# A two-layer block on one Trainium2 core: ranking in the routing stage, weight slabs by number, the last LN's rows spread by PE, the last halves one by one

## The chip, the cores and the metric

The kernel runs on one core of one Trainium2 chip. The metric is the device time of one execution in microseconds (us); lower is better. The engines are called as in the profile: PE (TensorE's matrix products; PEld is its weight loads), DVE (VectorE), ACT (ScalarE), POOL (GpSimd) and SP (SyncE, which here issues nearly all DMAs). TensorE's clock has two levels, 1.2 and 2.4 GHz; the profile gives the granted clock as a share of the full one.

## What is computed

256 tokens of width 1024 pass through two layers. The first is attention, retention and a dense feed-forward; the second, which is what matters here, is a mixer (gated delta rule and stick-breaking attention), an LN, a mixture of experts and a last LN:

```python
def second_block(x, meta_tokens, ...):
    ...
        mix = hybrid_mixer(h, ...)
        h = layer_norm_2(DEEPNORM_ALPHA * h + mix, ln1_g[i], ln1_b[i])
        ffn = hierarchical_moe(h, ...)
        h = layer_norm_2(DEEPNORM_ALPHA * h + ffn, ln2_g[i], ln2_b[i])
    return h[:, N_META:]

def hierarchical_moe(h, ...):
    ...
    g_idx = jnp.argmax(group_probs, axis=-1)
    ...
    top_logit, top_idx = lax.top_k(sel_logits, TOP_K_IN_GROUP)
    top_w = jax.nn.softmax(top_logit, axis=-1) * g_prob[:, None]
    ...
    for gi in range(N_GROUPS):
        hid = (jax.nn.silu(jnp.einsum("td,edf->tef", t, expert_w_gate[gi]))
               * jnp.einsum("td,edf->tef", t, expert_w_up[gi]))
        hid = hid * combine[:, gi, :, None].astype(hid.dtype)
        y = y + jnp.einsum("tef,efd->td", hid, expert_w_down[gi])
    return y.reshape(b, l, d)
```

Each token picks one of 4 groups and 2 of its 8 experts (D = 1024 in, 256 hidden). So there are 32 experts, each with gate and up weights (w_gu) and down weights (w_down), all in f32, and all of them are read from memory.

## The kernel before

**Weights and slots.** An expert has three slabs of 1 MB, 128 partitions of 2048 f32: two for w_gu (its first four and its last four blocks of 128 rows) and one for w_down. `expert_slot` (L1906) hands out slots in turn from a ring of 18: 11 of the pool "expert", 3 raw buffers, 4 more. The slab with number n lies where slab n - 18 lay, and its load waits until PE has read that one for the last time. `expert_part` (L1915) takes a slot and issues the load on SP at L1917.

**Passes.** `experts` (L1841) goes through the 32 experts in 10 passes. Passes 0 to 2 are static, two experts each (0 to 5), 64 token places each. The other 26 are ranked by how many tokens chose them: the two most chosen get one pass of two (pass 8), the rest passes of four with 32 places each (3 to 7, and 9 the last). So SP can't load a slab of a ranked expert until it knows its number: `ranked` in `passes` reads it from the tile ids with a `values_load` (L1827).

**One pass.** `expert_weights` (L1888) first takes the numbers of its experts, then issues their w_gu slabs, then the w_down slabs of the pass before. `gate_up` (L1987) multiplies, for k = 0 to 7, each expert's slab with the gathered tokens xT into the PSUM tile gu; between the products of some k it calls what the table `between` holds for it. Then come the down products of the pass before (`down`, L2013, into PSUM tiles dn, one for each half nh of 512 columns) with their weighting (`weighted`, L2023: yh on ACT, yl on DVE), `hidden` (L2001: Silu on ACT, a product on DVE, two transposes aT on PE), what `after` holds, and the scatter of the pass before (`scatter`, L2030: four products for each half, which add up in the PSUM tiles moe).

```python
1865                 between, after = {1: [g], 3: [r], 5: [r], 7: [self.weigh] if ranking else []}, [r]
```

g is a step of the gather of tokens (products xT<-P,hTh and xT<-P,hTl, and the PT turns), r a step of `ranking` (L1725). Its first step counts the tokens of each expert on PE (count and countc) and makes the order (perm) on DVE; the second turns the expert numbers into that order (ranked on PE, ids on DVE at L1754); further steps order the places and weights. `weigh` (L1678) makes the tokens' weights from the logits and touches Silu on ACT once, so that its table is there. From the start of the experts on, PE's products keep the order in which they are written.

**SP's queue.** SP issues in the order of the program; a load that waits for its slot holds up all that stand behind it. Ahead of the experts stand the loads of the mixers' weights and, among them, the slabs of passes 0 to 2.

**The end.** After pass 9 the last four w_down slabs, which `expert_weights` loads in halves (L1902, 512 KB each: all first halves, then all second), are multiplied: down of both halves, then for each half the scatter and `add_half` (L2036: two adds on DVE into the residual xh, L2041, which give the sums of the rows too). `last_norm` (L2079) loads the last LN's two rows of 1024 with two loads of 512 KB that spread each over the 128 partitions (L2085), and makes squares on ACT and the norm on DVE and POOL. `mm` (L323) and `transpose` (L331) are the helpers that issue PE's work.

Of the kernel before, what the change touches and what calls it, by code (L numbers as in the profile page):

```python
# [10 lines left out]
F32 = mybir.dt.float32  # L11
# [6 lines left out]
P = 128  # L18
D = 1024
# [10 lines left out]
STATIC, TOP = 6, 2  # L30
# [188 lines left out]
class Core:  # L219
# [1556 lines left out]
    def moe(self, xh, pl):  # L1776

        nc, ap = self.nc, self.ap
        hh, hl = self.hm = [self.keep([2, D], f"hT{s}", 1, dt=F32R) for s in "hl"]
        low = lambda eng, t, n: eng.tensor_tensor(hl[:, t, n], xh[t][:, n], hh[:, t, n].bitcast(F32), op=ALU.subtract)  # L1780
        half = [slice(nh * 512, (nh + 1) * 512) for nh in range(2)]
        nc.scalar.copy(hh[:, 0], xh[0])
        low(nc.gpsimd, 0, slice(0, D))
        with self.tc.issue_after(self.turned):
            for n in half:
                nc.scalar.copy(hh[:, 1, n], xh[1][:, n])
        last = self.choose(1, pl[1])
        self.counts(1)
        with self.tc.issue_after(last):
            low(nc.vector, 1, half[0])  # L1790
        passes, first = self.passes(), []
        for t in range(2):
            if t:
                self.places(t)
            first.append(self.select(passes[:2], t))
        with self.tc.issue_after(last):
            low(nc.vector, 1, half[1])
        acc = [[self.ps("moe", "acc") for _ in range(2)] for _ in range(2)]
        rows = []
        for n in half:  # L1800
            rows.append([self.work([512], f"row{x}", 2048) for x in "gb"])
            for r, x in enumerate(rows[-1]):
                nc.sync.dma_start(x, ap["rows"][8 + r:9 + r, n].to_broadcast([P, 512]))

        def residual(nh):

            n, (g, b) = half[nh], rows[nh]
            with self.tc.issue_after(self.turned):
                for x in xh:
                    nc.vector.scalar_tensor_tensor(x[:, n], x[:, n], ALPHA, g, op0=ALU.mult, op1=ALU.mult)  # L1810
                    nc.vector.scalar_tensor_tensor(x[:, n], b, ALPHA, x[:, n], op0=ALU.mult, op1=ALU.add)

        self.ordered = True
        self.experts(passes, acc, self.add_half(xh, acc), first, self.ranking(), residual)
        self.ordered, self.line = False, None
        self.last_norm(xh)
        self.overflow(xh)
# [23 lines left out]
    def experts(self, passes, acc, done, first=None, ranking=None, residual=None, eng=None):  # L1841

        n = len(passes)
        x, pg, at = [], {}, {}
        gathers = self.gathers(passes, x, first)
        g = lambda: next(gathers, None)
        for _ in range(4):
            g()  # L1850
        r = (lambda: next(ranking, None)) if ranking else (lambda: None)
        y = {}
        aT = dn = None

        def down(p, dn):
            for nh in range(2):
                y[p, nh] = self.weighted(self.down(aT, dn, nh), x[p][2])

        def scatter(p, nh):
            self.scatter(x[p][1], y.pop((p, nh)), nh, acc, p == 0, p == n - 1)  # L1860

        for p in range(n):
            w, dn, at[p] = self.expert_weights(passes[p][0], at.get(p - 1), eng)
            if p == 0:
                between, after = {1: [g], 3: [r], 5: [r], 7: [self.weigh] if ranking else []}, [r]
            elif p == 1:
                res = [partial(residual, nh) for nh in range(2)] if residual else [lambda: None] * 2
                between, after = {1: [res[0], g], 3: [g, g], 5: [g, g, res[1]], 7: [r]}, [g, g, r]
            else:
                between = {3: [g, g] if p % 2 else []}  # L1870
                after = [g, g] if p % 2 else [g, g, g]
            pg[p] = self.gate_up(x[p][0], w, between)
            if p:
                down(p - 1, dn)
            aT = self.hidden(pg.pop(p))
            for f in after:
                f()
            if p:
                for nh in range(2):
                    scatter(p - 1, nh)  # L1880
        p = n - 1
        _, dn, _ = self.expert_weights(None, at[p], eng)
        down(p, dn)
        for nh in range(2):
            scatter(p, nh)
            done(nh)

    def expert_weights(self, experts, before, eng=None):  # L1888


        ap, g, d, at = self.ap, None, None, None
        if experts is not None:
            at = [get() for get in experts]
            g = [[self.expert_part(ap["w_gu"][e, i], eng) for e in at] for i in range(2)]
        if before is not None:
            if experts is not None:
                return g, [self.expert_part(ap["w_down"][e], eng) for e in before], at
            d = [self.expert_slot() for e in before]
            for nh in range(2):
                n = slice(nh * 1024, (nh + 1) * 1024)  # L1900
                for a, e in zip(d, before):
                    (eng or self.nc.sync).dma_start(a[:, n], ap["w_down"][e, :, n].rearrange("o p n -> p (o n)"))  # L1902
            d = [a.rearrange("p (k n) -> p k n", k=4) for a in d]
        return g, d, at
# [108 lines left out]
    def down(self, aT, dn, nh):  # L2013

        n = len(dn)
        py = self.ps("dn")
        for j in range(2):
            for e in range(n):
                r = slice(P // n * e, P // n * (e + 1))
                self.mm(py[r, :], aT[:, j, r], dn[e][:, 2 * nh + j, :], j == 0, j == 1)  # L2020
        return py
# [23 lines left out]
    def overflow(self, res):  # L2045
# [5 lines left out]
        with tc.If(n > CAP):  # L2051
# [24 lines left out]
                        nc.vector.tensor_copy(a, tmp)  # L2076
            self.last_norm(res)

    def last_norm(self, res):  # L2079

        nc = self.nc
        x = self.expert_slot().rearrange("p (t n) -> p t n", t=2)
        gb = self.expert_slot().rearrange("p (t n) -> p t n", t=2)
        for i in range(2):
            nc.sync.dma_start(gb[:, i], self.ap["rows"][10 + i:11 + i, :].to_broadcast([P, D]))  # L2085
        g, b = gb[:, 0], gb[:, 1]
        halves = [slice(nh * 512, (nh + 1) * 512) for nh in range(2)]
        sq = self.expert_slot()[:, :D]
        for t in range(2):
            s = self.sums[t]  # L2090
            nc.vector.tensor_scalar(s[:, 2:3], s[:, 0:1], s[:, 1:2], -1.0 / D, op0=ALU.add, op1=ALU.mult)
            nc.scalar.activation(sq, res[t], AF.Square, bias=s[:, 2:3], accum_out=s[:, 3:4])
        for t in range(2):
            s = self.sums[t]
            nc.vector.scalar_tensor_tensor(x[:, t, :], res[t], s[:, 2:3], g, op0=ALU.add, op1=ALU.mult)
            nc.vector.tensor_scalar(s[:, 4:5], s[:, 3:4], 1.0 / D, EPS, op0=ALU.mult, op1=ALU.add)
            nc.gpsimd.tensor_tensor(s[:, 5:6], s[:, 4:5], self.mhalf[:, 0:1], op=ALU.pow)
        for t in range(2):
            for n in halves:
                o = x[:, t, n]  # L2100
                nc.vector.scalar_tensor_tensor(o, o, self.sums[t][:, 5:6], b[:, n], op0=ALU.mult, op1=ALU.add)
                nc.sync.dma_start(self.out[t * P:(t + 1) * P, n], o)
# [57 lines left out]
```

## Time and profile before

| | |
|---|---|
| median of three runs | 917.5 us (914.66 to 918.17) |
| the profiled execution's own time | 914.81 us |
| its span | 913.1 us |
| PE busy | 812.8 us, 89% of the span |
| PEld busy | 611.3 us, 67% |
| DVE busy | 511.7 us, 56% |
| ACT busy | 310.4 us, 34% |
| POOL busy | 117.2 us, 13% |
| mean granted clock of TensorE | 0.957 |
| moved by DMA | 218.10 MB, mean 239 GB/s |

All the views are of the profiled execution. The span is what the trace covers, and the times of rows are counted from its start. A busy share is a mean over stages that have different limits, so a row is read together with the stage that it lies in. Ends of matmuls are modelled, so distances between starts say more of PE than durations do.

### The profile page before, as it was taken

How to read it: one execution, taken by the hardware profiler on the slowest of the kernel's cores; microseconds unless marked ns; L12 is line 12 of the kernel's file. 1: busy time of each engine (PE TensorE's matmuls, PEld its weight loads, DVE VectorE, ACT ScalarE, POOL GpSimd, SP SyncE). 2: the span in 40 equal slices, each digit the busy share in tenths (PEclk: the TensorE clock that was granted, in tenths of full speed). 3: DMA queues.
4: the chain of work that ended last, by engine and by line, in shares of the span. 5: the costliest groups of instructions: out<-in, count | busy, mean ns of one | idle time of the engine just before them, and what ended most of it. 6: DMA issues, size and time to landing. Idle time of an engine off the chain costs nothing.

```text
span 913.1 us, 13514 instructions
## 1 busy us (share of the span) xinstructions
PE 812.8 (89%) x5311; PEld 611.3 (67%) x5311; DVE 511.7 (56%) x971; ACT 310.4 (34%) x491; POOL 117.2 (13%) x121
## 2 busy tenths in 40 slices
PE   4989789989999999889798999999988988866884
PEld 3886456668999998679797997899863443322321
DVE  4595748595655555845787458875655333120214
ACT  3343336354444444333463343544332211100101
POOL 0002400140000001452415201300010000000000
PEclk9999989989999999797999999999979999999987
DMA  8967546655755555033332130489655999999994
GB/s 310 365 230 299 209 185 253 232 192 180 254 185 189 185 192 193 24 127 136 136 139 84 42 108 13 145 339 335 264 229 244 421 414 421 421 421 421 422 416 179
DMA packets 35895, 218.10 MB, mean 239 GB/s; under 512 B 5976, under 2 KB 6496, under 8 KB 12144
## 3 DMA queue, kind: packets, MB, share of 16 engines
q1 hardware_dynamic: 33888, 215.09, 61.0%
q10 hardware_dynamic: 1936, 2.07, 0.8%
q8 instruction: 44, 0.72, 0.3%
q14 instruction: 27, 0.22, 0.1%
HBM read 216.09 MB, written 1.05 MB: 238 GB/s over the span
## 4 chain that ended last, share of the span: by engine, by line
PE 62%; DMA 17%; DVE 13%; ACT 4%; POOL 2%; issue 2%; SPq 0%; DVEq 0%; ACTq 0%; POOLq 0%
DMA expert<-in_w_down 8%; DMA raw<-in_w_gu 4%; PE gu L323 4%; PE ff L319 3%; PE ff L317 3%; PE ff L318 3%; PE f L319 3%; PE f L317 3%; PE f L318 3%; DMA expert<-in_w_gu 2%; PE dn L323 2%; PE Z L323 2%; PE xT L323 2%; PE y L318 2%; PE gate L317 2%
## 5 line engine op out<-in xcount | busy, mean ns | idle before, releaser
L300 DVE TENSOR_TENSOR lo<-raw,hi 128x1024 fp32r<-128x1024 f32 (+1 forms) x145 | 175.6, 1224 | 96.1 <-ACT hi L299 95.7
L299 ACT CAST hi<-raw 128x1024 fp32r<-128x1024 f32 (+1 forms) x155 | 156.6, 1028 | 176.7 <-PE ff L319 57.2
L323 PE MATMUL gu<-expert,xT 128*32 128x512 f32 (+1 forms) x424 | 81.4, 629 | 9.5 <-DMA expert<-in_w_gu 9.5
L317 PE MATMUL f<-hTh,hi 128*128 128x256 f32 x256 | 72.1, 282 | 0.0
L319 PE MATMUL f<-hTh,lo 128*128 128x256 f32 x256 | 71.8, 280 | 0.0
L318 PE MATMUL f<-hTl,hi 128*128 128x256 f32 x256 | 71.7, 280 | 0.0
L323 PEld LDWEIGHTS gu<-expert,xT 128*32 128x32 f32 (+1 forms) x424 | 20.0, 122 | 55.8 <-issue 36.4
L317 PE MATMUL ff<-hi,ffh 128*128 128x512 f32 x128 | 52.2, 408 | 4.4 <-DVE ffh L470 4.4
L323 PE MATMUL dn<-expert,aT 128*32 128x512 f32 (+1 forms) x224 | 46.9, 626 | 9.7 <-DMA expert<-in_w_down 9.7
L319 PE MATMUL ff<-hi,ffl 128*128 128x512 f32 x128 | 52.6, 411 | 2.0 <-DVE ffl L471 2.0
L318 PE MATMUL ff<-lo,ffh 128*128 128x512 f32 x128 | 52.2, 408 | 0.0
L318 PEld LDWEIGHTS f<-hTl,hi 128*128 128x128 f32 x256 | 48.2, 188 | 0.9 <-issue 0.2
L317 PEld LDWEIGHTS f<-hTh,hi 128*128 128x128 f32 x256 | 48.2, 188 | 0.9 <-issue 0.2
L319 PEld LDWEIGHTS f<-hTh,lo 128*128 128x128 f32 x256 | 48.3, 189 | 0.0
L2005 DVE TENSOR_TENSOR a<-gu,a 128x256 f32<-128x256 f32 x10 | 4.2, 422 | 72.8 <-ACT a L2004 72.8
L300 POOL TENSOR_TENSOR lo<-raw,hi 128x1024 fp32r<-128x1024 f32 x10 | 25.1, 2518 | 121.3 <-ACT hi L299 121.3
L323 PEld LDWEIGHTS dn<-expert,aT 128*32 128x32 f32 (+1 forms) x224 | 11.3, 121 | 39.4 <-issue 19.3
L317 PE MATMUL gate<-hTh,hi 128*128 128x256 f32 x128 | 37.4, 292 | 0.0
L2027 DVE SCALAR_TENSOR_TENSOR yl<-dn,s,yh 128x512 fp32r<-128x512 f32 x20 | 15.0, 749 | 38.8 <-ACT yh L2026 38.8
L323 PE MATMUL xT<-P,hTh 128*128 128x256 f32 x80 | 25.1, 339 | 12.7 <-ACT xT L1959 11.2
L319 PE MATMUL gate<-hTh,lo 128*128 128x256 f32 x128 | 36.1, 282 | 0.0
L318 PE MATMUL gate<-hTl,hi 128*128 128x256 f32 x128 | 36.0, 281 | 0.0
(597 smaller groups left out, 1981.0 us busy)
## 6 DMA issues: line engine op xcount, KB each, us to landing
expert<-in_w_gu SPq DMA_DIRECT2D x53, 1024.0 KB, 13.7
raw<-in_w_ff SPq DMA_DIRECT2D x32, 1024.0 KB, 4.8
expert<-in_w_down SPq DMA_DIRECT2D x24, 1024.0 KB, 19.7
raw<-in_w_in SPq DMA_DIRECT2D x22, 1024.0 KB, 4.8
raw<-in_w_gu SPq DMA_DIRECT2D x11, 1024.0 KB, 19.3
wa<-in_w_ada SPq DMA_DIRECT2D x8, 1024.0 KB, 8.7
raw<-in_w_gate SPq DMA_DIRECT2D x8, 1024.0 KB, 4.7
raw<-in_w_ada SPq DMA_DIRECT2D x8, 1024.0 KB, 4.8
```

Source lines behind the costliest of these rows:

```text
L299: nc.scalar.copy(h[:, :w], f)
L300: (nc.gpsimd if pool else nc.vector).tensor_tensor(l[:, :w], f, h[:, :w].bitcast(F32), op=ALU.subtract)
L317: mm(out, sh, mh, start=first, stop=False)
L318: mm(out, sh, ml, start=False, stop=False)
L319: return mm(out, sl, mh, start=False, stop=last)
L323: i = self.nc.tensor.matmul(out, lhsT, rhs, start=first, stop=last).ins
L2005: nc.vector.tensor_tensor(a, pg[:, FE:], a, op=ALU.mult)
L2027: nc.vector.scalar_tensor_tensor(yl, py, w[:, 0:1], yh.bitcast(F32), op0=ALU.mult, op1=ALU.subtract)
```

## The change

It has four parts.

1. `moe` makes the ranking and runs its first step (count, countc, perm) before `experts` begins, in the stage that routes the tokens. In pass 0 the second step stands after k = 1, with the gather's step, where it stood after k = 5; `weigh` stands after k = 5, where it stood after 7.
2. At pass 3 (where 2 * p == STATIC) `expert_weights` issues the w_down slabs of the pass before first, then reads the numbers and issues the w_gu slabs. Pass 2's w_down slabs become numbers 18 and 19 of the ring, and the w_gu slabs of pass 3 numbers 20 to 27; from number 28 on nothing is different.
3. `last_rows` loads the two rows of the last LN as 8 KB to one partition, in a tile of a work ring, and spreads them: four products with a row of ones in f32 into PSUM, and four copies on ACT. It is called in pass 9 after the gather's steps, ahead of the scatter of pass 8. The two broadcast loads are gone.
4. After the last pass, each half goes through down, weighting, scatter and add by itself.

```diff
@@ moe
+        ranking = self.ranking()
+        next(ranking)
         self.ordered = True
-        self.experts(passes, acc, self.add_half(xh, acc), first, self.ranking(), residual)
+        self.experts(passes, acc, self.add_half(xh, acc), first, ranking, residual)
@@ experts
-        def down(p, dn):
-            for nh in range(2):
+        def down(p, dn, halves=range(2)):
+            for nh in halves:
                 y[p, nh] = self.weighted(self.down(aT, dn, nh), x[p][2])
...
         for p in range(n):
-            w, dn, at[p] = self.expert_weights(passes[p][0], at.get(p - 1), eng)
+            w, dn, at[p] = self.expert_weights(passes[p][0], at.get(p - 1), eng, ranking and 2 * p == STATIC)
             if p == 0:
-                between, after = {1: [g], 3: [r], 5: [r], 7: [self.weigh] if ranking else []}, [r]
+                between, after = {1: [g, r], 5: [self.weigh] if ranking else []}, [r]
...
             else:
                 between = {3: [g, g] if p % 2 else []}
                 after = [g, g] if p % 2 else [g, g, g]
+                if ranking and p == n - 1:
+                    after.append(self.last_rows)
...
         _, dn, _ = self.expert_weights(None, at[p], eng)
-        down(p, dn)
         for nh in range(2):
+            down(p, dn, [nh])
             scatter(p, nh)
             done(nh)
 
-    def expert_weights(self, experts, before, eng=None):
+    def expert_weights(self, experts, before, eng=None, down_first=False):
 
 
         ap, g, d, at = self.ap, None, None, None
+        if down_first:
+            d = [self.expert_part(ap["w_down"][e], eng) for e in before]
         if experts is not None:
             at = [get() for get in experts]
             g = [[self.expert_part(ap["w_gu"][e, i], eng) for e in at] for i in range(2)]
         if before is not None:
             if experts is not None:
-                return g, [self.expert_part(ap["w_down"][e], eng) for e in before], at
+                return g, d or [self.expert_part(ap["w_down"][e], eng) for e in before], at
@@ last_rows, last_norm
+    def last_rows(self):
+
+        nc = self.nc
+        f = self.work([2 * D], "gb", 8192)
+        self.gb = f.rearrange("p (t n) -> p t n", t=2)
+        nc.sync.dma_start(f[0:1], self.ap["rows"][10:12, :].rearrange("(o t) n -> o (t n)", o=1))
+        for i in range(4):
+            pb = self.ps("row")
+            c = slice(512 * i, 512 * i + 512)
+            self.mm(pb, self.onesr.bitcast(F32)[0:1], f[0:1, c])
+            nc.scalar.copy(f[:, c], pb)
+
     def last_norm(self, res):
 
         nc = self.nc
         x = self.expert_slot().rearrange("p (t n) -> p t n", t=2)
-        gb = self.expert_slot().rearrange("p (t n) -> p t n", t=2)
-        for i in range(2):
-            nc.sync.dma_start(gb[:, i], self.ap["rows"][10 + i:11 + i, :].to_broadcast([P, D]))
-        g, b = gb[:, 0], gb[:, 1]
+        g, b = self.gb[:, 0], self.gb[:, 1]
```

On SP, before the experts' ranked slabs; first the order of before (L1917 issues a slab, L1803 rows of the residual, L1827 reads a number; the raw tiles are slabs of pass 2's w_gu):

```order
L1917 DMA raw_6638<-in_w_gu 128x2048
L1917 DMA raw_6640<-in_w_gu 128x2048
L1803 DMA rowg_6328<-in_rows 128x512
L1803 DMA rowb_6329<-in_rows 128x512
L1803 DMA rowg_6332<-in_rows 128x512
L1803 DMA rowb_6333<-in_rows 128x512
L1917 DMA expert_6642<-in_w_gu 128x2048
L1917 DMA expert_6644<-in_w_gu 128x2048
L1917 DMA expert_6646<-in_w_down 128x2048
L1917 DMA expert_6648<-in_w_down 128x2048
L1827 TENSOR_LOAD ids_6425
```

and that of the changed kernel:

```order
L1923 DMA raw_6638<-in_w_gu 128x2048
L1923 DMA expert_6731<-in_w_down 128x2048
L1923 DMA raw_6640<-in_w_gu 128x2048
L1923 DMA expert_6733<-in_w_down 128x2048
L1803 DMA rowg_6328<-in_rows 128x512
L1803 DMA rowb_6329<-in_rows 128x512
L1803 DMA rowg_6332<-in_rows 128x512
L1803 DMA rowb_6333<-in_rows 128x512
L1923 DMA expert_6642<-in_w_gu 128x2048
L1923 DMA expert_6644<-in_w_gu 128x2048
L1923 DMA expert_6646<-in_w_down 128x2048
L1923 DMA expert_6648<-in_w_down 128x2048
```

Pass 2's two w_down slabs (6731 and 6733), which stood behind the first eight ranked slabs, have moved ahead of the residual's rows.

On PE, in gate_up of pass 0; first before (the rows of gu are single products, four for two k of two experts):

```order
L323 MATMUL count_6398<-identr,onesr 128x32 x2
L323 MATMUL countc_6401<-onesr,identr 26x2 x2
L323 MATMUL gu_6378<-expert_6374,xT_6336 64x512
L323 MATMUL gu_6378<-expert_6376,xT_6336 64x512
L323 MATMUL gu_6378<-expert_6374,xT_6336 64x512
L323 MATMUL gu_6378<-expert_6376,xT_6336 64x512
L323 MATMUL ranked_6419<-perm_6411,cst_3549 1x26
L323 MATMUL ranked_6419<-perm_6411,s_962_6406 1x26
L331 MATMUL turned_6422<-ident,cst_3549 26x128 x2
```

and then the changed kernel, from the end of the gather's step on:

```order
L323 MATMUL ranked_6411<-perm_6349,cst_3549 1x26
L323 MATMUL ranked_6411<-perm_6349,s_956_6344 1x26
L331 MATMUL turned_6414<-ident,cst_3549 26x128 x2
L323 MATMUL gu_6395<-expert_6387,xT_6353 64x512
L323 MATMUL gu_6395<-expert_6389,xT_6353 64x512
L323 MATMUL gu_6395<-expert_6387,xT_6353 64x512
L323 MATMUL gu_6395<-expert_6389,xT_6353 64x512
L323 MATMUL gu_6395<-expert_6391,xT_6353 64x512
```

The products ranked, behind twelve gu products before, now stand behind the first four; count and countc have left this place for the one before the gather.

On PE, between pass 9's aT and the last down products, in the changed kernel (gb is the tile of the two rows, moe the scatter of pass 8):

```order
L331 MATMUL aT_7850<-ident,a_7847 128x128 x2
L323 MATMUL row_7857<-gb_7855,onesr 128x512
L323 MATMUL row_7860<-gb_7855,onesr 128x512
L323 MATMUL row_7863<-gb_7855,onesr 128x512
L323 MATMUL row_7866<-gb_7855,onesr 128x512
L323 MATMUL moe_6324<-yh_7834,PT_7707 128x512
L323 MATMUL moe_6326<-yh_7834,PT_7707 128x512
```

Before, moe followed aT at once; the eight products of moe and then the last dn products are the next in both. On SP the load of gb's one partition stands just ahead of the eight halves of the last w_down slabs.

## Rows read from the trace of the kernel before

**Rows 1.** The page's first line.

```profile
span 913.1 us, 13514 instructions
```

**Rows 2.** Chain that ended last: start, length, engine, tile or line.

```profile
886.67 10.22 DMA expert<-in_w_down
896.93 1.92 PE dn L323 x10
...
900.35 2.44 DVE xh L2041 x8
...
903.05 2.47 DVE expert L2095 x2
```

**Rows 3.** Windows: length, busy time of the engines, granted clock, DMA share, GB/s.

```profile
650.00:663.00 13.00, 13.00 (x62) 10.52 (x61) 6.50 (x10) 2.70 (x3) 0.56 (x1) 1.00 0.44 161
...
686.00:694.00 8.00, 6.53 (x35) 2.03 (x36) 4.68 (x30) 2.63 (x6) 0.00 (x0) 1.00 0.01 2
...
720.00:782.00 62.00, 54.72 (x378) 23.24 (x374) 18.32 (x59) 9.05 (x16) 0.00 (x0) 1.00 1.01 419
```

**Rows 4.** Timelines of PE, DVE and ACT, pass 0: start, length, instruction, idle before.

```profile
687.74 0.40 PE L323 MATMUL count<-identr,onesr 128*128 128x32 f32 x2
...
690.48 1.94 PE L323 MATMUL gu<-expert,xT 128*64 128x512 f32 x8
693.89 0.44 PE L331 MATMUL aT<-ident,a 128*128 128x128 f32 x2 [1.47 <-DVE a L2005]
...
690.27 0.17 DVE L1754 CAST ids<-ranked 1x26 int32<-1x26 f32 x1 [1.13 <-PE ranked L323]
...
691.70 1.28 ACT L2004 ACT_TABLE_LOAD   x1
692.99 0.38 ACT L2004 ACTIVATE a<-gu 128x256 f32<-128x256 f32 x1
```

**Rows 5.** Timeline of SP's DMA issues.

```profile
650.63 5.76 SPq L1917 DMA_DIRECT2D raw<-in_w_gu  x2
...
693.15 7.94 SPq L1917 DMA_DIRECT2D expert<-in_w_gu  x8
...
722.76 0.90 SPq L1917 DMA_DIRECT2D raw<-in_w_gu  x2
```

**Rows 6.** PE's waits, 694 to 782 (two rows), then 782 to 897.

```profile
PE xT L323 <- ACT xT L1959: 6.6, 10, 0.7
PE PT L323 <- DVE s L1982: 2.7, 2, 1.4
...
PE dn L323 <- DMA expert<-in_w_down: 9.7, 8, 1.4
```

**Rows 7.** DMAs issued at 693.15 and 722.76: KB each, us to landing.

```profile
expert<-in_w_gu SPq DMA_DIRECT2D x1, 1024.0 KB, 4.7
...
raw<-in_w_gu SPq DMA_DIRECT2D x1, 1024.0 KB, 6.2
```

**Rows 8.** Windows: first gu products of pass 1 alone, and a stretch of pass 9.

```profile
694.81:700.09 5.28, 5.28 (x16) 1.46 (x16) 0.00 (x0) 0.00 (x0) 0.68 0.96 403
...
879.19:886.02 6.83, 6.23 (x26) 1.19 (x27) 0.00 (x0) 0.00 (x0) 0.00 (x0) 0.50 1.00 414
```

**Rows 9.** Tile fT: four f32 products; duration min/median/max in ns, starts.

```profile
L323 PE MATMUL fT<-ident,brow x8: 585/588/692, 376.4 to 379.6; 8*128 8x512 f32 x8
```

**Rows 10.** Timeline of the end: PE, DVE and ACT from 881 on.

```profile
881.71 5.75 PE L323 MATMUL gu<-expert,xT 128*32 128x512 f32 x26 [0.57 <-DMA expert<-in_w_gu]
...
891.16 0.72 PE L323 MATMUL moe<-yh,PT 128*128 128x512 f32 x2
...
891.89 0.75 DVE L2027 SCALAR_TENSOR_TENSOR yl<-dn,s,yh 128x512 fp32r<-128x512 f32 x1
...
893.37 3.34 PE L323 MATMUL dn<-expert,aT 128*32 128x512 f32 x22
...
895.36 0.69 ACT L2026 ACTIVATE yh<-dn,s 128x512 fp32r<-128x512 f32 x1 [3.50 <-PE dn L323]
```

## The prediction

> **What bounds the kernel now.** The change touches only the last 260 us, so the views were read from the end backwards. The profiled execution took 914.81 us, of which 913.1 are the span [rows 1]. The chain of waits shows the end: a transfer of the last w_down halves that lands at 896.89, then PE's down products, VectorE's adds and the last LN [rows 2]. The windows by stage show why: from 720 to 782 us the DMA engines move 419 GB/s at a share of 1.01, so a slab of 1,048,576 bytes takes 2.50 us, and the stage cannot end before the slabs that are left have passed. The same windows show where those engines were idle: 161 GB/s from 650 to 663 us, and 2 GB/s from 686 to 694 [rows 3]. In that last gap SP waits for the rank numbers: VectorE writes ids at 690.27 [rows 4], and SP's first ranked load goes out at 693.15 [rows 5].
>
> The reader should see a second thing. From 694 to 782 us PE never waits for a DMA: its largest waits are for ScalarE and VectorE; only after 782 is a w_down load on top of its list [rows 6]. So up to 782 the slabs run ahead of PE, and what lets SP issue the next one is PE releasing a slot.
>
> **Earlier slabs.** Pass 2's two w_down slabs no longer stand behind the id loads; SP issues them beside the two loads that begin at 650.63 [rows 5], where the engines are less than half busy. Worth 2 x 2.50 = 5.0 us of stream. The rank products follow four gate_up products of pass 0 instead of twelve: eight products earlier, and eight are two groups of 1.94 [rows 4], so 3.9, with the counts' 0.40 some 4.3 us. SP then has the ids at about 686 and issues near 689. Without any other limit the stream would run 5.0 + 4.3 = 9.3 us ahead.
>
> It can't. The load at 722.76 waits for gate_up of pass 2 to release its slot, and it lands 6.2 us after issue; the load at 693.15, which found the engines empty, took 4.7 [rows 5, 7]. So only 1.5 us of backlog were left there: a stream that is 9.3 us ahead runs dry at this slot and restarts at 722.76 + 4.7. The end gains 1.5 us, plus whatever PE itself gains before 722.76. DMA: Bandwidth & Descriptors of the Trainium skill (Anatomy of one DMA) gives about 2.0 us plus bytes over 436 GB/s for one transfer that GpSimd issues; SP issues these, and the estimate of 4.4 us stands against the row's 4.7; by it the backlog was 1.8 and the sum 0.3 lower.
>
> **PE up to that slot.** Removed between gate_up products: count and countc, 0.40 [rows 4]. Added ahead of the gather: the same, half of it ahead of tile 1's logits, and four gather products that used to fill a wait for VectorE now come after place. I take the sum as 0; bounds +0.5 and -0.5. The Silu table load ends at 691.70 + 1.28 = 692.98 while gate_up ends at 690.48 + 1.94 = 692.42; weigh now stands two k earlier, so the table is there and Silu starts about 0.5 us earlier [rows 4]; I take 0.4. The wait of 1.47 before aT shrinks to about 1.0. Behind it the granted clock was 0.68 over the next sixteen product halves, which took 5.28 us [rows 8]; at the full level eight took 1.94 [rows 4], which makes sixteen 3.7 after the overlap of their ends. The level fell from 2.4 to 1.2 GHz after PE had stood idle for that 1.47; two waits in front of PT, 2.7 in all [rows 6], cost no level, for over 720 to 782 the granted clock is 1.00 [rows 3]. I take it that the level stays at 2.4 GHz, and 1.6 us are saved (bounds 0 and 1.6). PE reaches 722.76 about 0.4 + 1.6 = 2.0 us earlier, and the stream ends 1.5 + 2.0 = **3.5 us earlier** (bounds 1.0 and 4.0).
>
> **The last LN's rows.** Two broadcast loads of 512 KB go; they stand behind the last slab on SP and are first read after 903.05 [rows 2], so this is worth nothing. The one load of 8 KB takes their place ahead of the last w_down halves; 8 KB at 419 GB/s are 0.02 us, and the tile that it overwrites was last read in pass 7: nothing. What costs is PE. Four products of 128x512 in f32 stand between aT and the scatter of pass 8. The nearest row is another four products of 512 columns in f32, which show as eight halves with starts from 376.4 to 379.6 [rows 9]: 0.46 apart, 0.44 without the longer first one. Four products are 8 x 0.44 = 3.5 us. TensorE: Matmul & The Clock Gate of the Trainium skill (Back-to-back issue gap) has about 216 ns for one lone matmul of 512 columns at the full clock; taken for each half it makes an estimate of 1.7 us, and the sum 1.8 lower. Here the row decides.
>
> PE has no room for them: from 881.71 it runs without a wait to 887.46, then through dn, aT and moe; the first wait for a slab is 0.22, between 893.37 + 3.34 = 896.71 and 896.93 [rows 2, 10]. In before's times: aT is done at 891.16, product 1 runs to 892.04. Product 2 writes the PSUM bank of the second dn of pass 8, which VectorE reads until 891.89 + 0.75 = 892.64; so 892.68 to 893.56, then products 3 and 4 to 895.32. The eight scatter products took 893.37 - 891.16 = 2.21 with waits for yl that are now over [rows 10]; at 1.85 they end at 897.17. The last down products, at 893.37 before, start **3.8 us later** (3.0 to 4.5: yl's wait may be shorter, the products 0.46). ScalarE's four copies run beside this.
>
> **The halves one by one.** From that start to the last add it took 902.79 - 893.37 = 9.42 us before [rows 2, 10], with the last slab's landing inside. Now: down half 0 to its yh 1.99; yh and yl, 0.69 and 0.75 [rows 10], with the gaps between 1.47; scatter 2.21 / 4 = 0.55; the same 4.01 for half 1; two adds at 2.44 / 4 = 0.61 [rows 2]: 9.24. The two adds that half 0 takes away from the end are paid for by PE standing idle while yh and yl of half 0 are made. 0.2 is within the error of this sum: 0.0.
>
> **Sum.** -3.5 + 3.8 = +0.3 us against the profiled 914.81: 915.1. The median of the runs shown is 917.5, 2.7 above that execution, and they spread from 914.66 to 918.17; I forecast **917.8**. Differences under 0.5% (4.6 us) are what this measurement cannot tell from none.
>
> **Rivals.**
> - *The stream keeps its whole lead.* If slots didn't bind, -9.3 + 3.8 = -5.5: 912.0. For it: 419 GB/s and the chain. Against: 6.2 against 4.7 at 722.76. 0.12.
> - *The tail's additions hide.* If PE did the row products while it would wait for the last slabs, the tail would cost nothing: -3.5, 914.0. For it: those slabs land until 896.89 [rows 2]. Against: one wait of 0.22. 0.15.
> - *PE gains nothing early.* The level falls before pass 1 as now, the wait for aT being shorter but not gone: the stream gains 1.5 + 0.4, the tail costs 3.8, +1.9: 919.4. 0.13.
> - *Slower: the tail runs at 1.2 GHz.* Over 879.19 to 886.02 the granted clock was 0.50 [rows 8], after waits for slabs of up to 1.4 us [rows 6]. Such waits stay. With that level over the row, scatter and down products (3.5 + 1.85 + 1.7 of PE work from 891 on), this work doubles: +7.0, so 917.8 + 7.0 = 924.8. From 4.3 us of such work at the lower level on it decides the sign. Against: the fall came ahead of gate_up of pass 9, and PE is busy for 15 us after it. 0.10.
>
> **Chances.** The forecast itself, with stream gains of 2.5 to 4.0 and a tail of 3.0 to 4.5, keeps 0.50 and lies between 914 and 920 with the runs' spread. Faster by over 0.5%: the first rival and 0.02 of the second, 0.14. Slower: the last and 0.02 of the third, 0.12. The rest, 0.74, is no difference. The range holds the forecast's own, the second and the third rival, with the spread below 914.0 and above 919.4: 912.8 to 922.0. It leaves out most of the first and the last rival, together 0.2.
>
> **What would show it.** Right: two w_down loads at about 651 and 656; ids near 686 and the first ranked load near 689; the DMA engines idle again for some us between 700 and 722, and the load of raw slabs at about 721 landing 4.7 after issue; the granted clock at 1.00 from 694 to 698; the last slab's landing 3.5 earlier; four row products of 3.5 us after the last aT, and 15.2 us from the end of that aT to the last add, where it was 902.79 - 891.16 = 11.6. Wrong: a stream at 420 GB/s without a gap from 690 on (the first rival); PE waiting for a slab after its row products (the second); a granted clock of 0.5 in the tail (the last).

## The result and the profile after

The changed kernel takes 922.47 us (median of six runs, 920.72 to 924.62); the kernel before, measured beside it on the same chip, 915.87 (914.48 to 918.17). The ratio is 1.0072, its 95% interval 1.0051 to 1.0093: slower by 6.6 us, where 917.8 and no difference were forecast (the kernel before itself came out 1.6 below the 917.5 that the forecast was built on). It lies above the range (912.8 to 922.0), and two thirds of the way to the last rival, the tail at 1.2 GHz (924.8).

The profiled executions took 914.81 and 920.72 us, 5.9 apart, and their traces can be laid side by side. What stands ahead of the changed part varies by some us from one execution to the next, so the distances below are counted from a row that both have: SP's first load of the residual's rows, at 663.74 before and here at

```profile
664.52 0.33 SPq L1803 DMA_DIRECT2D rowg<-in_rows  x1
```

in the timeline of SP. The last aT on PE stands at 890.97 before (its first scatter product follows at 891.16 [rows 10]) and here, in the timeline of PE, at

```profile
889.26 0.44 PE L331 MATMUL aT<-ident,a 128*128 128x128 f32 x2
```

From the common row to this aT it takes 890.97 - 663.74 = 227.23 us before and 889.26 - 664.52 = 224.74 after: **2.5 us gained**. From that aT to the first product of the last LN on VectorE (903.05 before [rows 2], 908.88 after) it takes 12.08 before and 19.62 after: **7.5 us lost**. With the 0.8 by which the common row came later, this is the 5.8 between 903.05 and 908.88.

The chain that ended last, of the changed kernel (start, length, what), is to be laid beside [rows 2]:

```profile
865.82 19.82 DMA expert<-in_w_down
885.69 3.65 PE dn L323 x14
...
891.05 3.63 PE row L323 x6
894.68 3.71 PE moe L323 x8
898.39 2.58 PE dn L323 x16
...
908.88 2.48 DVE expert L2110 x2
```

Before, the last transfer handed over to the last ten down products. Now the transfer on the chain is one of pass 8's, and everything behind it is PE's own work, the row products among it. The reader should look at the lengths: eight scatter products (moe) take 3.71 us, where they took 2.21 [rows 10], and sixteen instructions of down products 2.58, where the other half's sixteen at the end take

```profile
903.26 1.90 PE dn L323 x16
```

The windows of the changed kernel say why (length, busy time of PE, PEld, DVE, ACT, POOL, granted clock, DMA share, GB/s):

```profile
886.07:892.90 6.83, 6.53 (x23) 2.24 (x20) 1.91 (x3) 2.54 (x4) 0.00 (x0) 1.00 1.03 410
892.90:899.73 6.83, 6.83 (x19) 3.09 (x21) 0.00 (x0) 1.17 (x2) 0.00 (x0) 0.50 0.17 68
899.73:909.97 10.24, 5.99 (x36) 1.73 (x28) 5.47 (x13) 2.62 (x4) 0.00 (x0) 1.00 0.01 2
```

In the middle of the row products the granted clock falls to 0.50, that is from 2.4 to 1.2 GHz, and it stays there for 6.83 us, though PE is busy all the time. In the kernel before, the window over its whole tail has 1.00 in this column:

```profile
886.02:903.09 17.07, 14.89 (x76) 5.30 (x68) 6.59 (x17) 3.23 (x6) 0.00 (x0) 1.00 0.70 276
```

At half the clock 6.83 us hold 3.4 us of work, so by this estimate 3.4 us are lost, on top of the row products themselves.

The early part, in the same order as [rows 3] to [rows 5]: the DMA engines now work where they were half idle, and there is a new hole further on.

```profile
650.00:663.00 13.00, 13.00 (x60) 10.49 (x60) 6.86 (x10) 2.86 (x4) 0.56 (x1) 1.00 0.82 322
...
720.00:725.00 5.00, 5.00 (x26) 1.69 (x24) 0.00 (x0) 0.07 (x1) 0.00 (x0) 1.00 0.48 169
735.00:740.00 5.00, 3.69 (x28) 2.22 (x20) 0.54 (x1) 1.13 (x2) 0.00 (x0) 1.00 0.96 351
```

The first window went from 161 to 322 GB/s; the second is the hole that was forecast at the slot of 722.76, and the third a smaller one, at the slot of 737.53, that wasn't. The timelines of PE and of SP show the other steps:

```profile
687.94 5.37 PE L323 MATMUL gu<-expert,xT 128*64 128x512 f32 x24
694.28 0.44 PE L331 MATMUL aT<-ident,a 128*128 128x128 f32 x2 [0.97 <-DVE a L2011]
```

```profile
691.01 20.46 SPq L1923 DMA_DIRECT2D expert<-in_w_gu  x9
...
721.45 0.90 SPq L1923 DMA_DIRECT2D raw<-in_w_gu  x2
```

The wait ahead of aT is 0.97 instead of 1.47, and the clock stays at the full level behind it. Counted from the common row, the first ranked load goes out at 26.49 us instead of 29.41, and the load at the slot of pass 2's gate_up at 56.93 instead of 59.02.

### The profile page after: what moved, and what is told of

It reads as the page before. It is cut to its first block, busy times and chain, and to the rows that moved or that the text cites. A ratio compares the mean times of both kernels' runs of the same rounds, so it can differ in the third digit from the quotient of the medians.

```text
span 919.1 us, 13531 instructions
## 1 busy us (share of the span) xinstructions
PE 819.0 (89%) x5319; PEld 615.1 (67%) x5319; DVE 511.8 (56%) x971; ACT 313.0 (34%) x495; POOL 117.3 (13%) x121
## 4 chain that ended last, share of the span: by engine, by line
PE 63%; DMA 16%; DVE 14%; ACT 4%; POOL 2%; issue 2%; SPq 0%; DVEq 0%; ACTq 0%; POOLq 0%
DMA expert<-in_w_gu 7%; PE gu L323 5%; DMA expert<-in_w_down 4%; PE ff L319 3%; PE ff L317 3%; PE ff L318 3%; PE f L319 3%; PE f L317 3%; PE f L318 3%; DMA raw<-in_w_gu 2%; PE dn L323 2%; PE Z L323 2%; PE xT L323 2%; PE y L318 2%; PE y L317 2%; PE y L319 2%
## 5 line engine op out<-in xcount | busy, mean ns | idle before, releaser
L323 PE MATMUL gu<-expert,xT 128*32 128x512 f32 (+1 forms) x424 | 78.8, 614 | 10.3 <-DMA expert<-in_w_gu 10.3
L323 PE MATMUL dn<-expert,aT 128*32 128x512 f32 (+1 forms) x224 | 49.9, 686 | 8.0 <-DMA expert<-in_w_down 8.0
```

Of the source, the lines that this page charges most:

```text
L323: i = self.nc.tensor.matmul(out, lhsT, rhs, start=first, stop=last).ins
```

## The experiments

Theory: the row products cost their own time at the end of PE's chain, and they bring the clock down besides; the early parts gain a little; the halves nothing. Rivals: the halves are the cost (1); the clock falls whatever stands there (2); the fall belongs to another part than the rows (3); the fall comes from PE's waits (theory B of two runs). The first four runs take the change apart. Beside the ratio, two distances of each trace: "to aT" (from the common row to the last aT) and "tail" (from the start of that aT to the last LN's first product).

| kernel | ratio to before, 95% interval | to aT | tail |
|---|---|---|---|
| before | 1 | 227.23 | 12.08 |
| the change | 1.0072 (1.0051 to 1.0093) | 224.74 | 19.62 |
| e1_no_rows | 0.9979 (0.9957 to 1.0002) | 224.70 | 12.22 |
| e2_rows_only | 1.0044 (1.0021 to 1.0067) | 226.75 | 16.06 |
| e3_halves_only | 0.9995 (0.9979 to 1.0012) | 226.91 | 12.21 |
| e4_early_only | 0.9989 (0.9964 to 1.0013) | 224.87 | 12.77 |
| e5_rows_pass8 | 0.9975 (0.9963 to 0.9988) | 223.94 | 12.22 |
| e6_rows_128deep | 1.0022 (1.0000 to 1.0045) | 224.20 | 16.29 |
| e7_rows_after_scatter | 1.0047 (1.0031 to 1.0064) | 226.33 | 19.99 |
| e8_ranking_only | 0.9987 (0.9973 to 1.0000) | 226.85 | 11.93 |
| e9_slabs_only | 0.9994 (0.9976 to 1.0012) | 225.56 | 12.75 |
| e10_rows_32deep | 1.0070 (1.0050 to 1.0091) | 225.15 | 19.64 |
| e11_no_halves | 1.0052 (1.0033 to 1.0071) | 225.32 | 17.68 |
| e12_128deep_no_halves | 1.0005 (0.9982 to 1.0028) | 227.05 | 14.40 |

The tails repeat within 0.9 us where the kernels have the same one (11.93 to 12.77 without row products). "To aT" does not: nine kernels have the changed early part and show 223.94 to 227.05, with 224.87 in the middle; the three with the early part of before show 226.75 to 227.23, 226.91 in the middle. So the early gain is about 2.0 us, and one trace alone says little of it. Part of the spread is the clock ahead of that aT: over pass 9's gate_up it was at 0.50 in the kernel before [rows 8], and it falls there in e7 and e12 too, which have the changed early part, but not in the changed kernel's execution. There the last run of gate_up's products is short (timeline of PE):

```profile
880.68 3.62 PE L323 MATMUL gu<-expert,xT 128*32 128x512 f32 x26 [1.45 <-DMA expert<-in_w_gu]
```

From its start to aT it takes 889.26 - 880.68 = 8.58 us, and 890.97 - 881.71 = 9.26 before [rows 10]: 0.7 of the 2.5 us gained comes from this.

**e1_no_rows.** The change, with the last LN's two broadcast loads as before:

```diff
-                if ranking and p == n - 1:
-                    after.append(self.last_rows)
...
-        g, b = self.gb[:, 0], self.gb[:, 1]
+        gb = self.expert_slot().rearrange("p (t n) -> p t n", t=2)
+        for i in range(2):
+            nc.sync.dma_start(gb[:, i], self.ap["rows"][10 + i:11 + i, :].to_broadcast([P, D]))
+        g, b = gb[:, 0], gb[:, 1]
```

> The change without last_rows: the two broadcast loads of the last LN are back, the ranking, the slabs by number and the halves stay. Theory (the row products cost 3.8 us of PE ahead of the last down products, and the granted clock's fall at 892.9 behind them another 3.4): the granted clock stays at 1.00 from 886 to the last scatter, the end of aT to the last LN's first product is 12 us again, and the time is that of before less the 1.1 us by which the last slab landed earlier: about 914.8, ratio 0.999. Rival 1 (the halves one by one cost the time, PE standing idle between them): 3 to 4 us above before, ratio 1.004. Rival 2 (the clock falls in the tail whatever stands there, since the slabs come earlier): 3.4 above before less 1.1, about 918.

Measured: the tail is 12.22 and the whole loss is gone; the median is 914.01, 2.4 below the kernel before on that chip, with an interval that just reaches no difference. Over the stretch that holds the whole tail the clock is 1.00:

```profile
886.00:899.90 13.90, 9.46 (x51) 3.84 (x50) 7.12 (x17) 3.45 (x6) 0.00 (x0) 1.00 0.55 215
```

So neither the halves nor the earlier slabs bring the clock down: rivals 1 and 2 fall (what the halves cost behind row products is a matter of e11 and e12).

**e2_rows_only.** The kernel before, with last_rows and its call alone.

> The kernel before with last_rows alone. Theory: the whole tail's loss and none of the early gain: 3.8 + 3.4 = 7.2 us above before, ratio 1.008, with the clock at 0.50 for about 7 us from the row products on. Rival 1 (the halves are the cost): no difference from before. Rival 3 (the row products alone cost their 3.8, the fall of the clock belongs to another part): 3.8 above, ratio 1.004, clock 1.00 there.

Measured: 1.0044, slower, with a fall of the clock behind the rows from 895.90 to 899.31, half as long as in the change. So the fall belongs to the rows, and rival 3 is wrong there, though the size is nearer to its 1.004 than to the theory's 1.008. The tail grows by 4.0 us, of which the fall is 1.7, so the products are left with 2.3, and not 3.8. The timeline of PE shows why: the last down products, which before ran from 893.37 to 898.85 between landing slabs [rows 2, 10], are one piece here, for the slabs have landed by the time the rows are done:

```profile
899.27 3.64 PE L323 MATMUL dn<-expert,aT 128*32 128x512 f32 x32
```

From there to the LN it takes 907.21 - 899.27 = 7.9 us, where it took 9.7 before.

**e3_halves_only.** The kernel before, with

```diff
-        down(p, dn)
         for nh in range(2):
+            down(p, dn, [nh])
             scatter(p, nh)
             done(nh)
```

> The kernel before with the last pass's halves one by one. Theory: 0.0 within 0.5 us, ratio 1.000; the second half's products wait for yl of the first, and the two adds of the first half leave the end. Rival 1: slower by 2 us or more. A gain is possible too, since the last slab lands only at 896.89 and the scatter of half 0 would use that wait: up to 1 us.

Measured: 0.9995 and a tail of 12.21: nothing, as the sum had it. From the last down products' start to the LN it takes 905.85 - 896.03 = 9.8 us, and 903.05 - 893.37 = 9.7 before. That 9.7 holds the waits for the last slabs, though; against the 7.9 of e2_rows_only, without them, the halves one by one would be 1.9 slower. e11 and e12 test that.

**e4_early_only.** e1_no_rows with the halves together again, so that only the early ranking and the slabs by number are left.

> The early ranking and the slabs by number alone, on the kernel before. Theory (slots released by PE bind up to 740 us): the time gains what PE gains before 722 us, 1.0 to 1.5 us, ratio 0.9985, with the stream idle between 700 and 722. Rival (the lead is kept when nothing else disturbs the stream): -9.3 us, ratio 0.990.

Measured: to aT 2.4 us less than before; the ratio, 0.9989, can't be told from 1, and 0.990 is out. The lead of 9.3 us is not kept: the prediction's first rival falls. The trace shows the restart as forecast: the load at the slot that bound at 722.76 lands 4.7 us after its issue, where it took 6.2 [rows 7]. The view of its DMA issue:

```profile
raw<-in_w_gu SPq DMA_DIRECT2D x1, 1024.0 KB, 4.7
```

**e5_rows_pass8.** The change, with the rows one pass earlier:

```diff
-                if ranking and p == n - 1:
+                if ranking and p == n - 2:
                     after.append(self.last_rows)
```

> The whole change, but last_rows is called in pass 8 (ahead of the scatter of pass 7) instead of pass 9. There PE waits for slabs in every pass from 782 us on. Theory (the rows cost only where PE has no wait to put them in): the 3.5 us of products take the place of waits for pass 9's w_gu slabs, the tail from the last aT to the last LN's first product takes 12 us as before, no fall of the clock behind 886; time of the run without the rows, 0.998 of before. Rival (the four products lower the clock wherever they stand, and gate_up of pass 9 at 1.2 GHz falls behind the slabs): ratio 1.002 or more.

Measured: 0.9975, clear of 1: 914.16 against 916.23 for the kernel before, and the lowest ratio of this study. The clock falls behind the rows there too, but PE has time for it, as the timeline of PE in pass 8 and a window over it show:

```profile
861.88 5.17 PE L323 MATMUL row<-gb,onesr 1*128 1x512 f32 x8
```

```profile
861.88:871.27 9.39, 9.38 (x21) 4.22 (x24) 1.57 (x10) 2.34 (x4) 0.00 (x0) 0.64 1.01 418
```

The eight halves take 5.17 us and the clock is 0.64 over the stretch; the DMA engines run at 418 GB/s all through it, and the tail is 12.22. Behind that the clock is 1.00 to the end of the tail, as the theory had it; the fall that the rival expected came in pass 8, but without the harm.

**e6_rows_128deep.** The change, with the same four products contracting over 128 partitions, 127 of them zero:

```diff
+        nc.gpsimd.memset(f, 0.0)
         nc.sync.dma_start(f[0:1], self.ap["rows"][10:12, :].rearrange("(o t) n -> o (t n)", o=1))
...
-            self.mm(pb, self.onesr.bitcast(F32)[0:1], f[0:1, c])
+            self.mm(pb, self.ident[:, 0:1].to_broadcast([P, P]), f[:, c])
```

> The whole change, but the four row products contract over all 128 partitions (column 0 of the identity as the weights, the tile's other 127 rows set to zero by GpSimd before the load) instead of one; the same four products of 512 columns in f32 at the same place. Theory A (the clock falls because products with one row of contraction leave nearly all of the array idle): the granted clock stays at 1.00 behind the rows, the end of aT to the last LN is 15.9 us instead of 19.6, ratio to before 1.003. Theory B (the fall comes from PE's waits around them or from the time of the rows alone): the fall is there as with one row, ratio 1.007.

Measured: no fall; theory A's 15.9 us came out as 16.29. The windows of this kernel over the rows, the scatter and the rest:

```profile
885.08:888.84 3.76, 3.27 (x10) 1.28 (x9) 1.16 (x2) 2.01 (x4) 0.00 (x0) 1.00 1.03 409
888.84:891.20 2.36, 2.36 (x10) 1.48 (x8) 0.00 (x0) 0.92 (x2) 0.00 (x0) 1.00 0.49 189
891.20:902.80 11.60, 6.71 (x41) 2.03 (x40) 6.08 (x14) 3.23 (x5) 0.00 (x0) 1.00 0.01 1
```

The rows' own place is 3.76 us long at the full level, and their wait for VectorE is still inside (timeline of PE):

```profile
886.59 2.81 PE L323 MATMUL row<-gb,ident 128*128 128x512 f32 x6 [0.49 <-DVE yl L2033]
```

The tail is 16.29 - 12.22 = 4.1 us longer than without the rows, and 19.62 - 16.29 = 3.3 shorter than with rows one deep. The 3.3 are the price of the clock.

**e7_rows_after_scatter.** The change, with the call of last_rows behind the scatter of pass 8 instead of ahead of it.

> The whole change, but the four row products stand behind the scatter of pass 8 instead of ahead of it, so that the second of them no longer waits for VectorE to leave its PSUM bank. Theory A (one row of contraction lowers the clock): the fall comes behind the rows again, over the last down products, ratio 1.006 to 1.008. Theory B (the wait of about 0.3 to 1.0 us in front of the second row product lowers it): no fall, ratio 1.003.

Measured: 1.0047; the rows run at 894.22 without a wait in front, and the clock falls from 897.26 to 907.50; the tail is 19.99. Theory B is out: the fall takes no wait ahead of the products. Nor do the waits for slabs ahead of aT explain it, which the changed kernel's execution has as well (1.45 us ahead of 880.68 and 0.38 ahead of 885.69): here PE is busy without a gap over the 10 us that end at the fall, as a window shows.

```profile
887.20:897.26 10.06, 10.06 (x39) 4.09 (x35) 2.35 (x4) 3.10 (x6) 0.00 (x0) 1.00 0.82 327
```

The ratio is below theory A's 1.006, by no more than the four runs of this kernel leave open (0.0017 to either side).

**e8_ranking_only** is e4_early_only without the w_down slabs ahead of the ids; **e9_slabs_only** is the kernel before with them alone.

> The early ranking alone on the kernel before: pass 2's w_down slabs stand behind the ids again. Theory (PE releasing slots binds the stream; PE's own gain is the clock that stays at 2.4 GHz behind pass 0's aT): all of the gain is here. Counted from the first load of the residual's rows, the first ranked load goes out 2.9 us earlier, pass 1's aT is 2.1 us earlier, the slabs at the end land 1.5 to 2.0 us earlier, as with both parts; ratio 0.998. Rival (the two parts' leads add up): half of what both give, 1 us.

> The slabs by number alone: pass 2's w_down slabs are issued ahead of the ids, the ranking stays in pass 0. Theory: PE gains nothing (the clock falls behind pass 0's aT as before), the load of pass 4's raw slab is issued when it was, the stream has at most 1.5 us of backlog to gain there and gives part of it back at the next slot: the last slabs land 0 to 1.0 us earlier; ratio 0.999 to 1.000. Rival (the leads add up): 1 us or more of the two parts' gain.

Measured: neither ratio can be told from 1, nor one from the other. To aT the ranking shows 0.4 us less than before and the slabs 1.7; with traces that differ by more than a us among themselves this does not decide between the theory and the leads adding up. What it does show: in e9 the clock falls behind pass 0's aT as before (697.31 to 700.72), in e8 it stays at 1.00, as in every kernel with the early ranking. But it does not fall in every execution of the ranking in pass 0 either. In e2_rows_only, whose early part is that of before, PE waits the same 1.47 us ahead of aT, and the clock stays at 1.00 behind it (timeline of PE, then a window):

```profile
695.23 0.44 PE L331 MATMUL aT<-ident,a 128*128 128x128 f32 x2 [1.47 <-DVE a L2007]
```

```profile
695.23:705.00 9.77, 9.00 (x46) 4.34 (x46) 6.13 (x21) 0.64 (x2) 0.00 (x0) 1.00 0.97 392
```

From this aT to the load at the slot of 722.76 it takes 27.16 us there, 27.17 in the change and 28.87 before. So the clock is worth 1.7 us at this place, and the early ranking gains them in those executions in which the clock would have fallen (three of the four traces with the ranking in pass 0). Why it falls in some alone, and how the rest of the gain is shared, stays open.

**e10_rows_32deep.** As e6_rows_128deep, over 32 partitions (the first 32 rows of the identity's column and of the tile).

> As the rows with 128 partitions of contraction, but with 32. If the clock follows how much of the array the products hold, 32 rows are a quarter and fall between: a fall behind the rows, perhaps a shorter one of 3.4 us (1.7 us of time), ratio 1.004; if any depth over one row is enough, no fall and ratio 1.002; if it needs the full depth, a fall of 6.8 us as with one row, ratio 1.006.

Measured: 1.0070, a tail of 19.64, and the fall in full, its window:

```profile
893.47:900.30 6.83, 6.83 (x22) 3.08 (x24) 0.00 (x0) 0.98 (x2) 0.00 (x0) 0.50 0.14 57
```

32 of the array's 128 rows do not keep the clock where all of them do. e6 and e10 differ in nothing but the depth (and in how many rows GpSimd sets to zero).

**e11_no_halves** is the change, and **e12_128deep_no_halves** is e6_rows_128deep, each with both down products of the last pass together again, as before.

> The change with both down products of the last pass together again, then both scatters. The row products delay the last down products until all slabs have landed; the two halves in one piece then take 7.9 us to the last LN in the run with the rows alone, while the halves one by one take 9.9 in the run with 128-deep rows. Theory (the halves cost nothing beside landing slabs, but 2.0 us behind row products): tail 17.6 us instead of 19.6 with a fall of 6.8 us, or 16.0 with one half as long; ratio 1.003 to 1.005. Rival (the halves cost nothing here either): tail 19.6, ratio 1.007.

> The change with 128-deep row products and both down products together: no fall of the clock, no halves. Theory: tail 16.3 - 2.0 = 14.3 us, 2.2 more than before, which the 2.4 us gained up to the last aT balance: ratio 1.000. Rival (the halves cost nothing here either): tail 16.3, ratio 1.002.

Measured: tails of 17.68 and 14.40, where 17.6 and 14.3 were expected; the rival's 19.6 and 16.3 are out. So the halves one by one cost 1.9 us behind the row products (19.62 - 17.68 and 16.29 - 14.40), though they cost nothing without them. The last down products of e12 are one piece again, in its timeline of PE, and its clock is at 1.00 from 888.00 to the last LN, as a window shows:

```profile
899.04 3.64 PE L323 MATMUL dn<-expert,aT 128*32 128x512 f32 x32
```

```profile
888.00:907.01 19.01, 16.49 (x80) 6.46 (x75) 6.54 (x16) 5.67 (x10) 0.00 (x0) 1.00 0.44 173
```

So two traces with products 128 deep show no fall in the tail, and all six with shallow ones show one behind them (the change, e2, e7, e10 and e11 in the tail, e5 in pass 8).

The tail's 7.5 us are thereby split: rows 14.40 - 12.08 = 2.3, halves 1.9, clock 3.3, each within the 0.9 by which tails repeat.

## Why the prediction was wrong

- **What bounds the kernel, and the slot at 722.76: right.** The load there went out at 56.93 us from the common row instead of 59.02, the DMA engines stood nearly idle ahead of it (25 GB/s from 720 to 721, and 169 over 720 to 725), and in e4_early_only it landed 4.7 us after issue. The first ranked load was 2.9 us earlier, not 4.3. The four gather products, which the forecast let cost nothing, now stand among the first four gate_up products and wait there for ScalarE's xT, so that these take 685.37 - 681.84 = 3.5 us, where they took 683.81 - 681.94 = 1.9 before (timeline of PE, changed kernel):

```profile
681.84 1.07 PE L323 MATMUL gu<-expert,xT 128*64 128x512 f32 x2
682.84 0.39 PE L323 MATMUL xT<-P,hTh 128*128 128x256 f32 x1
```

- **PE up to that slot: right in these two executions, and in part by luck.** "About 0.4 + 1.6 = 2.0 us earlier" was 0.4 + 1.7 = 2.1; the wait ahead of aT went to 0.97 and the clock stayed. But the kernel before had the fall in the execution that was read, and e2_rows_only shows that it need not come. Over all traces this load goes out at 57.99 to 59.02 us with the ranking in pass 0 and at 56.76 to 57.84 with the early ranking: 0.9 lies between the middle values.
- **The stream's end, 3.5 us earlier: too large, inside its bounds of 1.0 and 4.0.** The last half of a slab lands 231.31 us from the common row in e1_no_rows and 231.48 in e4_early_only, 233.15 before: 1.8 earlier. At the last aT the two profiled executions differ by 2.5, 0.7 of it from the clock in pass 9, and the middle of all traces by 2.0. What failed there is that only the slot at 722.76 counts: at the next, 737.53, the stream ran short a second time (351 GB/s from 735 to 740). The hole is measured; why a slab in it landed 3.4 us behind the one ahead of it, where it took 2.5 before, stays open. One 16 KB instruction packet passes in that stretch and may hold up one of the engines; no run tested it.
- **The last LN's rows 3.8, the halves 0.0: the sum was nearly right by luck, the shares were not.** Without the clock the two cost 16.29 - 12.08 = 4.2. The rows delay the last down products by about the forecast 3.8 (in e6, aT to them takes 891.20 - 884.81 = 6.39 against 893.37 - 890.97 = 2.40: 4.0), but 1.7 of that replaces waits for the last slabs, so that they cost 2.3. The eight scatter products behind them took 2.36 at the full level there, not 1.85. "PE has no room for them" looked only at the one wait of 0.22 and missed that the down products ran in pieces, 5.48 us for 3.64 of work. The halves then take the 1.9 back: with the slabs there, PE waits for yh and yl of half 0, where both down products in one piece would have covered them. The second rival (the tail's additions hide) was thus half right for the rows, and the change's own last part undid it.
- **The price of one f32 product: right.** e6 shows the eight halves in 3.76 us with a wait of 0.49 inside. By the Trainium skill's figure for one matmul (TensorE: Matmul & The Clock Gate, Back-to-back issue gap), which the prediction set beside its row, they would have taken half of that; the measurement decides for the row.
- **The clock of the tail: the step that failed and decided.** The prediction gave the fall to 1.2 GHz a chance of 0.10 and held against it that "PE is busy for 15 us after it". It looked for falls behind idle PE only. This one came while PE was busy, from the row products themselves, and cost 3.3 us. The kernel before held a sign of it: behind the very products of [rows 9] that gave the price, which contract over 8 rows, the clock falls too, as two of its windows show.

```profile
376.45:380.15 3.70, 3.70 (x9) 1.39 (x8) 3.70 (x4) 2.07 (x3) 1.88 (x1) 1.00 0.00 0
380.90:387.60 6.70, 6.02 (x26) 4.76 (x30) 5.96 (x8) 2.41 (x4) 5.47 (x4) 0.50 0.01 4
```

All fourteen traces have a fall there. A wait of PE of 1.4 us begins at the end of those products, so that place alone doesn't tell which of the two brings the clock down. For the sum of the change: without the clock's price the profiled executions differ by -2.5 + 4.2 = +1.7, ratio 1.002, which is what e6_rows_128deep shows; with it, by +5.0 from the common row on. So the clock decided between no difference and slower.
- The last rival had the right place and sign. Its cause (waits for slabs) is not the one that decided, and the level was low for 6.83 us, not for the whole tail.

What removed the loss is the move to pass 8 (e5_rows_pass8): there PE has waits to spare, and no cost of the rows is to be seen. Whether it is better than e1_no_rows, whose LN rows come by DMA behind the slabs, can't be told (0.9975 and 0.9979).

## What to carry to other kernels

Work that was moved from a DMA queue to an engine was free here only in a stage where that engine waits: the same four products, with the clock that they cost, took 5.6 us at the end of PE's chain and nothing that could be measured one pass earlier. Parts of a change are to be priced together, since a rearrangement that is free beside a wait (the halves) costs once another part has filled that wait. A product that spreads one row over the partitions kept PE busy here, and yet the clock fell, so look at the granted clock behind every shallow product on the path that sets the end.

## What the runs showed of the hardware

- Products that contract over 1 or 32 partitions brought the granted clock from 1.00 to 0.50 while PE was busy (in the changed kernel 6.53 us of the stretch from 886.07 to 892.90, and all of the fall itself; in e7_rows_after_scatter all 10.06 us ahead of it); the same products over 128 partitions, 127 of them zeros, did not. It is the depth of the product and not its values that counted here. TensorE: Matmul & The Clock Gate of the Trainium skill (HAM oscillation) gives idle gaps of PE as what brings the level down; here no idle longer than 0.30 us stood between the last aT and the fall:

```profile
891.05 3.63 PE L323 MATMUL row<-gb,onesr 1*128 1x512 f32 x6 [0.30 <-DVE yl L2033]
```

- The depth costs no time in itself: at the full clock the halves of the row products start 0.43 us apart both 128 deep (e6, 887.10 to 888.38) and one deep (e7, 894.75 to 896.90), about what the f32 halves of [rows 9] showed.
- The stream of loads ran short more than once: nearly dry at the slot that bound before (169 GB/s over 5 us), and again at the next (351 GB/s), which it now reached earlier. A lead is to be followed through every slot to the end of the stage.
